# Decoder trunk on one core: where the first layer's mixer issues its modulation steps

## The chip, the cores and the metric

One core of one Trainium2 chip. The time is that of one execution in device microseconds (us). TensorE is PE (its weight loads PEld), VectorE DVE, ScalarE ACT, GpSimd POOL, and SP the engine from which nearly all DMA transfers are issued. Every engine, and SP's DMA queue, takes its instructions in the order in which they are written.

## The reference

Two layers on x of 256 tokens x 2048, f32. Per layer, with `mod` a product of a condition vector with a 2048 x 12288 matrix:

```python
mod = silu(c) @ w_ada[l] + b_ada[l]           # 6 x 2048: shift, scale, gate for mixer and FFN
u = x * (1 + sc_m) + sh_m
proj = u @ w_in[l]
y_attn = sliding_window_attention(q, k, v, sinks, cos, sin)   # 16 heads, 4 kv heads, window 128, rotary
y_rwkv = rwkv7_group(proj[..., ATTN_COLS:], ...)              # 16 heads of 64, delta rule with decay
mix = concatenate([y_attn, y_rwkv]) @ w_out[l]
x = layer_norm(alpha * x + gt_m * mix)
u = x * (1 + sc_f) + sh_f
gate, up = split(u @ w_gate_up[l])
x = layer_norm(alpha * x + gt_f * ((silu(gate) * up) @ w_down[l]))
```

## The kernel before

**Streams.** Every weight is read once, in slabs of 128 rows x 1024 (or 512) columns. A slab is loaded into `raw` (L372), ACT casts its rounded part `hi` (L380), DVE takes the remainder `lo` (L381), and PE multiplies in three products (L402, L403, L405 into `acc`, or L414 to L416 with the operands turned). PE's order is: projection `w_in`, `w_out`, `w_gate_up`, `w_down`, then the second layer.

**Modulation steps.** The matrix `w_ada` (2 x 2048 x 12288) isn't multiplied on PE, except for a small first part. It is worked off in 20 units of 1024 columns, each of 16 steps and three empty turns. A step is one load of 128 x 1024 f32 (512 KB) into `ast`, which has two buffers (L253), and one DVE instruction that multiplies by a scalar per partition and adds to `aacc` (L257, the first of a unit L255). After the 16 steps and two empty turns the unit is summed over partitions: eight PE transposes (L277), eight ACT instructions that add up rows (L281), one DVE instruction (L284) that writes `mods`; gates are written out too (L289). The units are in a fixed order over both layers, and what is not taken in one place is taken in the next.

Steps are drawn from this list in three ways: `pump()` at each weight slab, at `AP[l]` (mixer), `AO[l]` (output projection) and `AF_[l]` (FFN) steps a slab; `adv(n)` at given places, n at a time: `AR` for each of the four chunks of a recurrence, `AA` for each of the 12 operations of attention; and `need()`, which draws what is still wanted before its use.

**The mixer's order.** It is written out in `ORDER`, one string a layer. The RWKV heads are in four groups (0 to 3): D decays, R projection, A preparation (L627 to L720: `ssb` L644, `rs` L647, `rb` L654, `aa` L681, `am` L684, `ax` L692, `at` L699, `kb` L710), I inverse (L723 to L757), C recurrence (L760 to L830), E close. The inverse goes through DRAM: `am` is written to `nscr`, read as `nb` (L727), inverted in 16 x 16 blocks on POOL (L733, L735), written to `tinv` (L738), read as `tm` (L741), then refined in two levels, each of `ytr` (DVE, L745), a product (PE, L749), `yx`, and a product (PE, L756). Q is the projection of q, k, v, X a swap of buffers; a, b and c are attention's rotate, weigh and gather for each kv head (`qk` L888, `ra` L894, `rb` L895, `qr`; scores, softmax `pr` L932; sums into `yl` L460); w and z give the finished columns to `w_out`. For the first layer:

```python
"D0 R0 A0 D1 I0 R1 C0 E0 Q1 A1 I1 D2 R2 A2 Q0 D3 C1 R3 E1 I2 A3 X Q2 a0 a1 b0 C2 a2 b1 c0 E2 a3 c1 I3 b2 b3 c2 c3 w0 C3 w1 w2 E3 z0 z1 z2 z3 w3"
```

The program is then put through a list scheduler that gives each engine its final order by its own estimate of times; so an edit in one place can turn the order of instructions far from it. In the first layer the recurrences 0 and 1 lie beside weight slabs of the projection; 2 and 3 and attention lie mostly behind the last of these slabs.

Of the kernel before, what the change touches and what calls it, by code (L numbers as in the profile page):

```python
# [45 lines left out]
LAG = 2  # L46
WB = (4, 3, 2)
RED = 1
AR = (3, 7)
AA = (1, 45)  # L50
AP = (0.65, 0.3)
AO = (1.1, 2.9)
AF_ = (0.75, 0.55)
# [14 lines left out]
def hybrid_trunk_kernel(  # L68
# [21 lines left out]
    def bank(name="mb", tag="mb"):  # L90

        if tag == "cb":
            return ps.tile([P, 512], F32, tag="cb", name=name)
        t = f"m{turn[0]}"
        turn[0] ^= turn[1]
        return ps.tile([P, 512], F32, tag=t, name=name, bufs=1)
# [241 lines left out]
    def adv(n):  # L338
        for _ in range(n):
            next(ada_rest, None)  # L340
# [149 lines left out]
    def mixer(l, us, mixp, feeds):  # L490
# [71 lines left out]
        def have_y(kts):  # L562
            for k in kts:
                if ys[k] is None:
                    yf = pool_of("ysc").tile([P, T], F32, tag="ysc", name="yf", bufs=1)
                    dma(yf, yd[l, k])
                    ys[k] = split_y(yf)
# [192 lines left out]
        def recur(g, st):  # L760
# [43 lines left out]
            sb = [None, None]  # L804
            H2 = [slice(64 * h, 64 * h + 64) for h in range(2)]
            for cc in range(NCH):
                adv(AR[l])
                o = cc * P
                if cc > 0:
                    for i in I2:  # L810
                        PE.matmul(ob[BH[i], o:o + P], lhsT=st[i]["rh"][:, cc - 1, :], rhs=sb[i], start=True, stop=False)
                for h in range(2):
                    for i in I2:
                        PE.matmul(ob[BH[i], o + h * CH:o + (h + 1) * CH], lhsT=st[i]["am"][h][:, cc, CH:],
                                  rhs=st[i]["uv"][:, cc, H2[h]], start=(cc == 0), stop=(cc == 0 or h == 1))
                if cc == NCH - 1:
                    break
                db = bank("db", "cb")
                for i in I2:
                    for h in range(2):  # L820
                        PE.matmul(db[H2[h], i * CH:(i + 1) * CH], lhsT=st[i]["bkt"][:, cc, H2[h]], rhs=st[i]["uv"][:, cc, H2[h]],
                                  start=True, stop=(cc == 0))
                    if cc > 0:
                        for h in range(2):
                            PE.matmul(db[H2[h], i * CH:(i + 1) * CH], lhsT=st[i]["mt"][:, cc - 1, H2[h]], rhs=sb[i][:, H2[h]],
                                      start=False, stop=True)
                sn = states[turn_s[0]]
                turn_s[0] ^= 1
                for h in range(2):
                    S.copy(sn[H2[h], :, H2[h]], db[H2[h], 0:2 * CH].rearrange("p (i s) -> p i s", i=2))  # L830
                sb = [sn[:, i, :] for i in I2]
# [183 lines left out]
        for op in ORDER[l].split():  # L1015
# [3 lines left out]
            if op[0] == "D":  # L1019
                st[n] = decays(n)  # L1020
            elif op[0] == "R":
                bks[n] = project(n)
            elif op[0] == "A":
                nscr[n] = prepare(n, st[n], bks[n])
            elif op[0] == "I":
                invert(n, st[n], nscr[n])
            elif op[0] == "C":
                recur(n, st[n])
            elif op[0] == "E":
                close(n, st[n])  # L1030
            elif op[0] == "Q":
                project_qkv((AW, 0, 512)[n])
            elif op[0] == "X":
                if not COEX[l]:
                    pa_cm.__exit__(None, None, None)
                    pt_cm, pt = open_pt()
            elif op[0] == "a":
                rotate(n)
            elif op[0] == "b":
                weigh(n)  # L1040
            elif op[0] == "c":
                gather(n)
            elif op[0] == "w":
                add_attention([2 * n, 2 * n + 1], op == ORDER[l].split()[-1])
            elif op[0] == "z":
                add_heads(n, op == ORDER[l].split()[-1])
            if op[0] in "abc":
                adv(AA[l])
        have_y(range(KT))
# [302 lines left out]
```

## Time and profile before

| | |
|---|---|
| three runs | 2692.5, 2694.9, 2695.86 us; median 2694.9 |
| profiled execution | 2694.28 us, of which the span 2692.6 |
| mean granted TensorE clock | 0.965 |
| busy share PE, DVE, ACT, POOL | 93%, 68%, 44%, 5% |
| share of the 16 DMA engines' time taken by SP's transfers (q1) | 71.6% |
| first layer's attention, first `ra` to last `yl` | 448.8 to 537.5 us |
| second layer's | 1772.1 to 1844.9 us |

A busy time is the sum over an engine's instructions. Matmuls overlap in the profile, so their ends are modelled. A bracket behind an instruction gives the idle time of its engine just before it, and what ended it; `x2` joins two alike. A link of the chain is the instruction, transfer or wait that the next one needed last.

### The profile page before, as it was taken

The numbers are of one execution on the slowest core, as the hardware profiler recorded it, in microseconds if no ns is written. First come the engines' busy times: TensorE is split into PE (matmuls) and PEld (weight loads), VectorE is DVE, ScalarE is ACT, GpSimd is POOL, SyncE is SP. The second block draws the span as 40 slices with busy tenths as digits, with TensorE's granted clock in tenths as the row PEclk, the third lists the DMA queues.
The fourth block names the chain that finished last, engine by engine and source line by source line (L and its number), as shares of the span: only waits on it lengthen the run. The fifth ranks groups of instructions, "written<-read, shape, count | busy, mean of one in ns | idle before, by whom it ended". The sixth has DMA issues, their size and how long they took to land.

```text
span 2692.6 us, 41752 instructions
## 1 busy us (share of the span) xinstructions
PE 2501.1 (93%) x15325; PEld 2093.1 (78%) x15325; DVE 1841.0 (68%) x2469; ACT 1188.3 (44%) x2029; POOL 135.0 (5%) x355
## 2 busy tenths in 40 slices
PE   3788998788999999999999999979899999999997
PEld 2687886567888888888889877867688888888887
DVE  6866767979877777777788677555764545545456
ACT  2364452435444444444445544534444444344442
POOL 1002112000000000000000022110000000000000
PEclk9789998899999999999999999989999999999999
DMA  9968668688998888889878586424756656666654
GB/s 315 381 188 253 198 191 238 180 317 296 353 330 309 297 303 312 293 295 308 308 263 304 174 259 188 117 72 144 253 172 188 190 186 196 195 189 189 193 188 149
DMA packets 351999, 637.49 MB, mean 237 GB/s; under 512 B 75894, under 2 KB 142898, under 8 KB 350258
## 3 DMA queue, kind: packets, MB, share of 16 engines
q1 hardware_dynamic: 351794, 634.82, 71.6%
q8 instruction: 120, 1.97, 0.3%
q14 instruction: 85, 0.70, 0.1%
HBM read 622.08 MB, written 12.62 MB: 236 GB/s over the span
## 4 chain that ended last, share of the span: by engine, by line
PE 68%; DMA 8%; DVE 6%; ACT 2%; issue 1%; POOL 1%; SPq 0%; DVEq 0%; POOLq 0%; ACTq 0%
PE acc L403 19%; PE acc L402 19%; PE acc L405 19%; DMA ast<-in_w_ada_dram 3%; DVE aacc L257 2%; PE acc L414 2%; PE acc L415 2%; PE acc L416 2%; DVE lo L381 1%; DMA raw<-in_w_gate_up_dram 1%; PE mb L1225 1%; DMA raw<-in_w_out_dram 1%; DMA yf<-yd 1%; PE mb L277 1%; ACT pr L947 0%
## 5 line engine op out<-in xcount | busy, mean ns | idle before, releaser
L380 ACT CAST hi<-raw 128x1024 fp32r<-128x1024 f32 (+2 forms) x728 | 758.5, 1044 | 1110.8 <-PE acc L405 833.1
L381 DVE TENSOR_TENSOR lo<-raw,hi 128x1024 fp32r<-128x1024 f32 (+2 forms) x728 | 880.2, 1212 | 519.8 <-PE acc L403 347.1
L403 PE MATMUL acc<-lo,u 128*128 128x512 f32 x1568 | 513.4, 395 | 11.9 <-DVE lo L381 11.8
L405 PE MATMUL acc<-hi,u 128*128 128x512 f32 x1568 | 505.8, 391 | 0.0
L257 DVE SCALAR_TENSOR_TENSOR aacc<-ast,cond,aacc 128x1024 f32<-128x1024 f32 x300 | 384.1, 1280 | 127.8 <-DMA ast<-in_w_ada_dram 126.6
L402 PE MATMUL acc<-hi,u 128*128 128x512 f32 x1568 | 457.2, 393 | 0.9 <-ACT u L360 0.5
L403 PEld LDWEIGHTS acc<-lo,u 128*128 128x128 f32 x1568 | 293.8, 189 | 76.4 <-DVE lo L381 16.2
L402 PEld LDWEIGHTS acc<-hi,u 128*128 128x128 f32 x1568 | 294.9, 188 | 63.4 <-ACT sg L1218 0.9
L405 PEld LDWEIGHTS acc<-hi,u 128*128 128x128 f32 x1568 | 295.2, 188 | 61.8 <-issue 0.5
L403 PE MATMUL acc<-lo,ht 128*128 128x512 f32 (+1 forms) x720 | 243.6, 377 | 3.0 <-DVE lo L381 2.9
L405 PE MATMUL acc<-hi,ht 128*128 128x512 f32 (+1 forms) x720 | 242.2, 375 | 0.0
L414 PE MATMUL acc<-u,hi 128*128 128x256 f32 x720 | 206.1, 293 | 14.0 <-ACT hi L380 14.0
L402 PE MATMUL acc<-hi,ht 128*128 128x512 f32 (+1 forms) x720 | 217.0, 376 | 0.0
L415 PE MATMUL acc<-u,hi 128*128 128x256 f32 x720 | 204.5, 291 | 0.0
L416 PE MATMUL acc<-u,lo 128*128 128x256 f32 x720 | 193.1, 294 | 7.1 <-DVE lo L381 7.1
L403 PEld LDWEIGHTS acc<-lo,ht 128*128 128x128 f32 x720 | 135.0, 188 | 29.3 <-DVE lo L381 5.6
L414 PEld LDWEIGHTS acc<-u,hi 128*128 128x128 f32 x720 | 141.9, 197 | 19.3 <-ACT hi L380 14.9
L405 PEld LDWEIGHTS acc<-hi,ht 128*128 128x128 f32 x720 | 135.6, 188 | 24.2
L402 PEld LDWEIGHTS acc<-hi,ht 128*128 128x128 f32 x720 | 134.8, 188 | 24.4
L415 PEld LDWEIGHTS acc<-u,hi 128*128 128x128 f32 x720 | 141.7, 197 | 2.6 <-issue 1.6
L416 PEld LDWEIGHTS acc<-u,lo 128*128 128x128 f32 x720 | 133.8, 197 | 11.6 <-DVE lo L381 9.0
L1067 POOL TENSOR_TENSOR brs<-brs,mhalf 128x1 f32<-128x1 f32 x8 | 7.6, 955 | 1698.7 <-DVE brs L1066 772.1
(349 smaller groups left out, 2901.1 us busy)
## 6 DMA issues: line engine op xcount, KB each, us to landing
ast<-in_w_ada_dram SPq DMA_DIRECT2D x368, 512.0 KB
raw<-in_w_gate_up_dram SPq DMA_DIRECT2D x704, 256.0 KB
raw<-in_w_down_dram SPq DMA_DIRECT2D x176, 512.0 KB
raw<-in_w_in_dram SPq DMA_DIRECT2D x82, 512.0 KB
raw<-in_w_out_dram SPq DMA_DIRECT2D x64, 512.0 KB
raw<-in_w_in_dram SPq DMA_DIRECT2D x120, 256.0 KB
ast<-in_w_ada_dram SPq DMA_DIRECT2D x32, 256.0 KB
lnw<-in_ln_w_dram SPq DMA_DIRECT2D x4, 1024.0 KB
```

The source lines that it names most:

```text
L257: ins = V.scalar_tensor_tensor(acc, t, cond[:, j:j + 1], acc, ALU.mult, ALU.add)
L277: PE.transpose(b[:, i * P:(i + 1) * P], blocks[q + i], ident)
L380: S.copy(h, fl)
L381: ins = V.tensor_tensor(r, fl, h.bitcast(F32), ALU.subtract)
L402: PE.matmul(bt, lhsT=xh, rhs=hi[:, c0:c0 + w], start=st, stop=False)
L403: PE.matmul(bt, lhsT=xh, rhs=lo[:, c0:c0 + w], start=False, stop=False)
L405: PE.matmul(banks[t][q][:, 0:w], lhsT=xl, rhs=hi[:, c0:c0 + w], start=False, stop=sp_)
L414: PE.matmul(bt, lhsT=hi[:, c0:c0 + w], rhs=xh, start=st and opens, stop=False)
L415: PE.matmul(bt, lhsT=hi[:, c0:c0 + w], rhs=xl, start=False, stop=False)
L416: PE.matmul(bt, lhsT=lo[:, c0:c0 + w], rhs=xh, start=False, stop=sp_ and closes)
L1067: G.tensor_tensor(rs[:, 0:1], rs[:, 0:1], mhalf[:, 0:1], ALU.pow)
L1225: PE.transpose(b[:, i * T + t * P:i * T + (t + 1) * P], hh[t][:, (2 * k2 + i) * P:(2 * k2 + i + 1) * P], ident)
```

## The change

In the first layer, each chunk of recurrences 0 and 1 draws six steps in place of three, and each chunk of recurrences 2 and 3 none. Attention's operations draw none in place of one. In the second layer nothing of this changes: seven for each chunk, 45 for each attention operation (by then the list is empty).

```diff
-AR = (3, 7)
-AA = (1, 45)
+AR = ((6, 6, 0, 0), (7, 7, 7, 7))
+AA = (0, 45)
...
             for cc in range(NCH):
-                adv(AR[l])
+                adv(AR[l][g])
```

So these places of the first layer draw 12 + 12 + 12 + 12 and 12 steps before, 24 + 24 + 0 + 0 and 0 after: 48 for 60. The list counts empty turns too. By the program's order, the counts of DVE steps (320 in all) ahead of some places are, before and after: `uv` (L780) of the recurrences 0 to 3 23, 32, 48, 68 and 23, 43, 64, 69, first `ra` 50 and 66, end of attention 79 and 69, first norm 98 and 89, and in the second layer `uv` of recurrence 0 311 and 297. Of PE's rows, 378 matmuls stand between the last one of the second layer's projection and the first of its `w_out` before, 540 after. On DVE in the second layer, group 1's `rs` stood 25 rows ahead of recurrence 0's `uv` (L780), and now stands 28 rows behind it.

SP, first layer, at the start of attention: `nb`, `tinv` and `tm` are group 3's inverse, `qk` and `vt` the rotation's operands, `qkv` the projection's result. Before:

```order
L727 DMA nb<-nscr 64x16x16
L253 DMA ast<-in_w_ada_dram 128x1024 x2
L888 DMA qk<-qkv 128x2x256
L889 DMA qk<-qkv 128x2x64
L876 DMA qkv<-stg 128x512
L890 DMA vt<-qkv 128x2x64 x2
L253 DMA ast<-in_w_ada_dram 128x1024
L890 DMA vt<-qkv 128x2x64
L253 DMA ast<-in_w_ada_dram 128x1024
```

and, five rows further on, after another `qk`, `L738 DMA tinv_154<-ttl 64x8x16 x2`. After:

```order
L253 DMA ast<-in_w_ada_dram 128x1024
L727 DMA nb<-nscr 64x16x16 x2
L253 DMA ast<-in_w_ada_dram 128x1024 x2
L738 DMA tinv_154<-ttl 64x8x16 x2
L741 DMA tm<-tinv_154 64x8x64 x2
L888 DMA qk<-qkv 128x2x256
L889 DMA qk<-qkv 128x2x64
L876 DMA qkv<-stg 128x512
L890 DMA vt<-qkv 128x2x64 x2
```

The inverse's way through `tinv` and `tm` moved ahead of the rotation's first load.

DVE at the same place: the rows at the second rotation before, where group 3's first `ytr` stands (the first rotation's `ra` is ten rows above):

```order
L894 TENSOR_TENSOR ra<-qk,cosk 128x640
L895 TENSOR_TENSOR rb<-qk,sink__147 128x640
L898 TENSOR_TENSOR qr<-ra,rb 128x5x32
L899 TENSOR_TENSOR qr<-ra,rb 128x5x32
L898 TENSOR_TENSOR qr<-ra,rb 128x5x32
L899 TENSOR_TENSOR qr<-ra,rb 128x5x32
L257 SCALAR_TENSOR_TENSOR aacc<-ast,cond,aacc 128x1024
L854 TENSOR_TENSOR sq<-os__4848,vr 128x512
L257 SCALAR_TENSOR_TENSOR aacc<-ast,cond,aacc 128x1024
L745 STREAM_TRANSPOSE ytr<-tm 128x512
```

and the rows at the first rotation after:

```order
L798 TENSOR_TENSOR mt<-mr,mt 128x256
L800 TENSOR_TENSOR rh<-mr,ar 128x192
L720 TENSOR_TENSOR bv<-bnb,vx 128x256
L745 STREAM_TRANSPOSE ytr<-tm 128x512
L255 TENSOR_SCALAR aacc<-ast,cond 128x1024
L257 SCALAR_TENSOR_TENSOR aacc<-ast,cond,aacc 128x1024
L894 TENSOR_TENSOR ra<-qk,cosk 128x640
L895 TENSOR_TENSOR rb<-qk,sink__147 128x640
```

`ytr` moved from behind the second rotation to ahead of the first.

PE, second layer, at the end of the projection (L402, L403, L405 with `u` are its matmuls; L769 to L825 are a recurrence). Before, its last rows, and what follows:

```order
L402 MATMUL acc<-hi,u 128x512
L403 MATMUL acc<-lo,u 128x512
L405 MATMUL acc<-hi,u 128x512
L718 MATMUL bnb<-xr,bones 128x256
L769 MATMUL ta<-atl,tm 64x64 x7
L775 MATMUL tk<-uv,tm 64x64 x16
L784 MATMUL mr<-bkt,ah 128x128 x2
L791 MATMUL mr<-am,ah 64x64 x6
```

After, the last `L405 MATMUL acc<-hi,u 128x512` is followed by the rest of recurrence 1 and some sums, 19 rows, and then:

```order
L845 MATMUL gb<-gda,g2a 128x256
L846 MATMUL gb<-gdb,g2b 128x256
L277 MATMUL mb<-ident,aacc 128x128 x4
L644 MATMUL ssb<-bones,kkn 64x2 x8
L289 MATMUL mb<-ident,mods_136 8x128
L654 MATMUL rb<-ident,rs 64x64 x16
L858 MATMUL oc<-ident,sq 128x128 x4
L681 MATMUL aa<-ar,bkc 128x128 x8
L749 MATMUL m_16800<-ytr,am 64x64 x10
L681 MATMUL aa<-ar,bkc 128x128 x4
```

Group 3's preparation (L644, L654, L681) and the inverse of group 2 (L749) moved from among the projection's matmuls to behind the last of them.

## The prediction

> **What bounds the kernel now.** I read the page's totals first, then the chain that ended last, then the windows around the two places where the edit changes how many steps run, and there the chain and the timelines of single engines.
>
> ```profile
> span 2692.6 us, 41752 instructions
> PE 2501.1 (93%) x15325; PEld 2093.1 (78%) x15325; DVE 1841.0 (68%) x2469; ACT 1188.3 (44%) x2029; POOL 135.0 (5%) x355
> PE 68%; DMA 8%; DVE 6%; ACT 2%; issue 1%; POOL 1%; SPq 0%; DVEq 0%; POOLq 0%; ACTq 0%
> L257 DVE SCALAR_TENSOR_TENSOR aacc<-ast,cond,aacc 128x1024 f32<-128x1024 f32 x300 | 384.1, 1280 | 127.8 <-DMA ast<-in_w_ada_dram 126.6
> ```
>
> PE is busy for 93% and carries 68% of the chain, so where weight slabs stream, a step (one load of `ast`, one DVE instruction of 1.28 us) hides behind matmuls. DMA and DVE carry 14% of the chain; those are the stretches without a stream. The windows (columns: length, then PE, PEld, DVE, ACT and POOL busy, the granted clock, DMA share, GB/s) show which:
>
> ```profile
> 447.00:540.00 93.00, 68.82 (x668) 52.30 (x666) 82.37 (x210) 40.69 (x146) 10.32 (x11) 0.82 0.66 191
> 1772.00:1843.00 71.00, 58.82 (x574) 44.48 (x574) 44.78 (x170) 30.07 (x107) 2.79 (x5) 0.79 0.08 22
> 1730.00:1763.00 33.00, 33.00 (x359) 26.95 (x357) 18.72 (x29) 11.37 (x15) 9.06 (x30) 1.00 0.43 117
> 1763.00:1772.00 9.00, 3.72 (x73) 3.03 (x72) 2.94 (x7) 1.52 (x5) 0.00 (x0) 0.97 0.81 236
> 1600.00:1660.00 60.00, 53.92 (x578) 44.85 (x577) 46.42 (x72) 26.43 (x56) 17.77 (x34) 0.94 0.71 213
> ```
>
> The first two rows are the same stage, attention beside the last recurrences, in the first and the second layer. The first layer's has steps in it: DVE is busy 82.37 of 93 us and PE only 68.82. The second layer's has none: PE is busy 58.82 of 71. Row three is the end of the second layer's projection, where PE has no gap; row four is the wait behind it, PE 3.72 of 9. Row five lies around the second layer's first recurrence.
>
> **The change, part by part.** *First layer, last two groups and attention.* Here 12+12 steps of recurrences 2 and 3 and 12 of attention go, and 24 are added to recurrences 0 and 1, so that 12 fewer run in this layer's mixer, and the program order leaves 3 steps between the first rotation and attention's end. Cost of the 29 steps in the window, from the groups of its lines, and three of the chain's links there (start, length, link):
>
> ```profile
> L257 DVE SCALAR_TENSOR_TENSOR aacc<-ast,cond,aacc 128x1024 f32<-128x1024 f32 x29 | 37.1, 1281 | 10.2 <-DMA ast<-in_w_ada_dram 10.1
> 419.76 5.15 DMA ast<-in_w_ada_dram
> 448.93 5.83 DMA ast<-in_w_ada_dram
> 538.62 1.28 DVE aacc L257
> ```
>
> The steps take 37.1 us of DVE and 10.2 of waits, and their loads are links of the chain. How much of that is on the path is told by the stage's length with and without steps, from the first `ra` (rotation) to the last `yl` of attention, in the DVE timeline (start, length):
>
> ```profile
> 448.82 0.83 DVE L894 TENSOR_TENSOR ra<-qk,cosk 128x640 f32<-128x640 f32 x1
> 537.08 0.41 DVE L460 TENSOR_TENSOR yl<-acc,yl 128x256 fp32r<-128x256 f32 x1
> 1772.07 0.82 DVE L894 TENSOR_TENSOR ra<-qk,cosk 128x640 f32<-128x640 f32 x1 [0.49 <-DMA qk<-qkv]
> 1844.46 0.42 DVE L460 TENSOR_TENSOR yl<-acc,yl 128x256 fp32r<-128x256 f32 x1 [0.44 <-ACT yl L459]
> ```
>
> First layer 537.49 − 448.82 = 88.7 us; second layer 1844.88 − 1772.07 = 72.8. So the most that the removed steps can give is 88.7 − 72.8 = 15.9 us. I don't count on it, since with the steps gone the order turns at the stage's head. Before, SP issues the rotation's `qk` ahead of the last group's `tinv` and `tm` (the inverse, through DRAM), and DVE does `ra` ahead of `ytr`; now `tinv` and `tm` come ahead of `qk`, and `ytr`, which waits for `tm`, ahead of every `ra` (SP's rows in the section on the change). So attention starts when that inverse has come back from DRAM:
>
> ```profile
> 439.55 0.42 SPq L888 DMA_DIRECT2D qk<-qkv  x1
> 451.48 1.72 SPq L738 DMA_DIRECT2D tinv<-ttl  x2
> 427.34 1.28 DVE L684 TENSOR_TENSOR am<-aa,amask 128x512 f32<-128x512 f32 x2
> 464.27 0.71 DVE L745 STREAM_TRANSPOSE ytr<-tm 128x512 f32<-128x512 f32 x1
> 1741.34 1.29 DVE L684 TENSOR_TENSOR am<-aa,amask 128x512 f32<-128x512 f32 x2 [2.32 <-PE aa L681]
> 1770.87 0.71 DVE L745 STREAM_TRANSPOSE ytr<-tm 128x512 f32<-128x512 f32 x1 [4.94 <-DMA tm<-tinv]
> ```
>
> From `am`'s end to `ytr`'s start this group takes 464.27 − 428.62 = 35.7 us; the second layer's takes 1770.87 − 1742.63 = 28.2. By the first, `ytr` ends at 464.98, by the second at 457.5. I take 463, nearer to the group's own row. Then 72.8 us of attention, and the three steps that remain, 3 × 1.28 = 3.8 (estimates): 539.6 against 537.5, **+2**. Ends: 457.5 + 72.8 = 530.3 (−7), and 464.98 + 76.6 + 5.83 for one step's load in the path = 547.4 (+10). Queued behind the waiting `ytr` are all of the rotation, and behind that PE's scores.
>
> *First layer, recurrences 0 and 1.* Each issues 12 steps more, while a stream runs. SP has room there, and PE has a gap from a late `lo`:
>
> ```profile
> 356.90 1.12 SPq L372 DMA_DIRECT2D raw<-in_w_in_dram  x2
> 370.89 1.28 SPq L738 DMA_DIRECT2D tinv<-ttl  x2
> 379.72 0.38 PE L416 MATMUL acc<-u,lo 128*128 128x256 f32 x1 [2.55 <-DVE lo L381]
> ```
>
> The 12.9 us between the first two are free for loads. The new order has `lo` ahead of `ytr`, so that gap can go (−2.5); recurrence 0 stands some 1 us longer with 12 × 1.28 = 15.4 us more on DVE in front of its chain's end. Sum **−1.5**, ends −2.5 and +5 (four steps uncovered, 4 × 1.28).
>
> *First layer's FFN.* With 10 steps less behind it, the modulation unit for the second half of the FFN's input is summed inside the FFN's first stream, not ahead of the norm. ACT's part (same window, groups of lines):
>
> ```profile
> L281 ACT ACTIVATE mb<-mb 128x128 f32<-128x128 f32 x12 | 3.2, 263 | 4.9 <-PE mb L277 4.8
> L281 ACT ACTIVATION_READ_ACCUMULATOR mb<-mb 128x1 f32 x12 | 2.3, 190 | 0.0
> ```
>
> 8 × (263 + 190) ns = 3.6 us of ACT, while PE has the first half's matmuls: **+2**, ends 0 and +5 (3.6 and one more step's 1.28).
>
> *Second layer.* Ten of the twelve steps come back here, and by the order 23 instead of 9 lie beside its first recurrence, while the stream runs. In the fifth window DVE has 46.42 us busy of 60; 14 × 1.28 = 17.9 more make 64.3, 4.3 too many. Nor does DMA hide them: 60 us × 213 GB/s plus 14 × 0.524 MB is 20.1 MB, 335 GB/s, which is above what this window in another stream reached:
>
> ```profile
> 640.00:700.00 60.00, 55.32 (x246) 44.03 (x247) 53.70 (x72) 38.55 (x69) 1.30 (x2) 0.93 0.86 296
> ```
>
> At 296 GB/s it is 67.9, +7.9. I take **+5** for the stream, ends 0 and +12.9 (17.9 with 5 covered).
>
> The greater part is order. Before, group 1's preparation (DVE `rs`) stood ahead of recurrence 0; now it stands behind it with steps between, ten weight slabs later, and all behind it follows: group 3's preparation and two levels of group 2's inverse stood among the projection's matmuls, and now stand behind the last of them (PE's rows in the section on the change). 378 matmuls stood between the projection's last one and the first of w_out; now 540. The chain before, at the place where they hid (x counts loads and matmuls), and from DVE's timeline the start of the preparation and the end of a rotation:
>
> ```profile
> 1727.62 1.02 PE ssb L644 x16
> 1736.48 1.42 PE aa L681 x16
> 1728.65 1.08 PE m L749 x32
> 1728.69 0.17 DVE L647 TENSOR_SCALAR rs<-ssb 64x16 f32<-64x16 f32 x1 [0.52 <-PE ssb L644]
> 1774.38 0.32 DVE L899 TENSOR_TENSOR qr<-ra,rb 128x160 f32<-128x160 f32 x1
> ```
>
> The stream loses 162 small matmuls; at 58.82 us / 574 = 0.102 us each (the window of 1772) that is 16.6 us, and its end moves from 1763 to 1763 − 16.6 + 5 = 1751.4. From group 3's `rs` to `ytr` it was 1770.87 − 1728.69 = 42.2 us, beside a PE without a gap; now that chain begins where the stream ends: 1793.6. Two of the four rotations now come ahead of `ytr`; one took 1774.70 − 1772.07 = 2.6 us, so the stage gets −5.3: its start is at 1788.3 as against 1772.07, **+16.2** with the stream's +5 in it. Ends: with this stream gone the chain could go as fast as 42.2 − 16.6 = 25.6, which gives 0; with the tail of recurrence 1 and of group 2's inverse, some ten links of 1.08, in front of it, and the stream's upper end 7.9 more, 16.2 + 10.8 + 7.9 = +35. I take the middle, since the chain's own links are DVE, DMA and PE in turn, and only PE's lose their company.
>
> *Sum:* −1.5 + 2 + 2 + 16.2 = +18.7 on the profiled execution's 2694.28 us (span 2692.6), which is 0.6 under the median 2694.9: **2713 us**.
>
> [...] The windows give the clock as 0.79 where PE was busy 58.82 of 71 us and 1.00 where it had no gap. [...]
>
> GpSimd's part of the last group's inverse, in its timeline:
>
> ```profile
> 446.59 0.22 POOL L733 TENSOR_TENSOR tmp<-nb,ttl 128x21 f32<-128x21 f32 x1
> 447.75 1.22 POOL L733 TENSOR_TENSOR tmp<-nb,ttl 128x14 f32<-128x14 f32 x1
> 447.62 1.28 DVE L257 SCALAR_TENSOR_TENSOR aacc<-ast,cond,aacc 128x1024 f32<-128x1024 f32 x1
> ```
>
> The second took 1.22 us for fewer elements, and ended only when the step beside it did. [...]
>
> **The rivals.** *Faster: the first layer's tail is freed.* If `ytr` is not what attention waits for (the point: `ytr` ending by 449), the stage takes 72.8 us from 448.82 and ends at 521.6, −15.9; with no loss in the second layer, its tail's shorter chain making up for the moved work, and +2 at the FFN: 2680. For it: DVE's 82.37 of 93 us and the links of `ast`. Against: the orders on SP and DVE, and that the inverse took 28 us even without steps. *Same:* the second layer gives 0, its lower end, and the first −1.5 + 2 + 2: 2697. *Slower still:* the 14 steps of the second layer's stream are not covered at all, 17.9 instead of 5: 2726; for it, the `ast` waits that total 126.6 us on the page; against, that these lie mostly where PE runs on. That the edit does nothing is excluded: the rows moved on every engine.
>
> **How the numbers follow.** About 0.2% (5.4 us) is what a measurement of this kernel can tell from no change. Forecast (2703 to 2724) 0.58; slower still 0.12; same 0.12; faster 0.18. So slower 0.70. The range leaves out the faster case and reaches from 2686 (the first layer's lower end −7 with the second at 0) to 2730 (slower still and some more at the FFN).
>
> **What would show it.** After: first `ra` of the first layer at about 463 behind `ytr`, attention's end at 535 to 547; PE with one wait or several of 15 to 25 us in sum behind the second layer's last projection matmul, then attention of about 73 us. Wrong it would be if `ra` starts before 452, if attention ends before 528, or if the time from the first layer's end to the second layer's first w_out slab does not grow.

## The result, and the profile after

The changed kernel takes 2741.2 us (median of four runs, 2737.1 to 2749.4) against 2693.7: ratio 1.0178, interval 1.0163 to 1.0194. It is slower, as forecast, but by 47 us where 19 were forecast, and outside the range (2686 to 2730). The profiled execution took 2737.09 us, 42.8 more than the one before; all stages below are read from these two executions.

The page's totals:

```profile
span 2735.4 us, 41759 instructions
PE 2524.9 (92%) x15325; PEld 2109.7 (77%) x15325; DVE 1842.2 (67%) x2469; ACT 1188.1 (43%) x2029; POOL 134.3 (5%) x355
```

The same work is done: DVE is busy for the same time, and PE's busy time is 23.8 us more for the same 15325 matmuls. The rest is waiting and order. How late the changed kernel is at some places (start of an instruction in the timeline, after less before):

| place | before, us | late by |
|---|---|---|
| 51st `lo` of all (first layer, before recurrence 0) | 257.3 | −3.2 |
| 81st `lo` (first layer's projection, near its end) | 413.0 | +14.5 |
| end of attention (last `yl` from `acc`) | 537.5 | +4.5 |
| first residual of `w_out`, L1144 | 588.5 | +8.1 |
| second norm, third L1067 | 1400.4 | +12.3 |
| second layer, first `ra` | 1772.1 | +38.9 |
| its first residual, L1144 | 1889.7 | +44.8 |
| end of span | 2692.6 | +42.8 |

So the first layer loses 12.3 us (14.5 and more in its projection, of which attention gives back 10), and the second 30.5.

*The first layer's projection.* DVE's groups for the stretch from recurrence 0 to just behind the 81st `lo`, in the kernel before and in the changed one (busy time, mean ns, idle before and what ended it); the stretch is 275 to 420 us before, 275 to 435 after:

```profile
L381 DVE TENSOR_TENSOR lo<-raw,hi 128x1024 fp32r<-128x1024 f32 x30 | 36.3, 1214 | 11.1 <-PE acc L416 10.7 <-issue 0.4
L257 DVE SCALAR_TENSOR_TENSOR aacc<-ast,cond,aacc 128x1024 f32<-128x1024 f32 x21 | 26.7, 1270 | 2.5 <-DMA ast<-in_w_ada_dram 2.4
```

```profile
L257 DVE SCALAR_TENSOR_TENSOR aacc<-ast,cond,aacc 128x1024 f32<-128x1024 f32 x36 | 46.0, 1276 | 19.2 <-DMA ast<-in_w_ada_dram 18.9
L381 DVE TENSOR_TENSOR lo<-raw,hi 128x1024 fp32r<-128x1024 f32 x29 | 35.2, 1216 | 6.0 <-ACT hi L380 3.4 <-PE acc L416 2.6
```

Fifteen steps more are 19.3 us more of DVE and 16.5 us more of waits for their loads. Before, DVE waited 10.7 us for PE to free the next `lo`, that is PE was the bound; after, 2.6. SP's queue over 275 to 435, first before, then after (total wait, times, longest; for the kernel before this reaches 15 us past its stretch, and up to 420 its two rows are 44.1 and 8.8):

```profile
SPq L372 <- DVE lo L381: 45.6, 22, 6.8
SPq L253 <- DVE aacc L257: 11.1, 12, 1.7
```

```profile
SPq L253 <- DVE aacc L257: 26.4, 23, 2.8
SPq L372 <- DVE lo L381: 24.0, 17, 3.6
```

The weight loads (L372) used to wait 45.6 us in all for a free buffer; by so much they were ahead of DVE, which is called their lead here. Now the step's load (L253) waits 26.4 us for one of its two buffers, and the weights queue behind it; their lead is 24.0.

*The first layer's attention*, the windows and DVE's rows of its start:

```profile
435.00:470.00 35.00, 20.66 (x286) 17.03 (x284) 16.73 (x23) 9.13 (x30) 7.04 (x30) 0.82 0.59 173
470.00:542.00 72.00, 61.46 (x568) 46.10 (x570) 49.81 (x177) 31.07 (x112) 3.75 (x5) 0.78 0.20 61
```

```profile
467.66 0.71 DVE L745 STREAM_TRANSPOSE ytr<-tm 128x512 f32<-128x512 f32 x1 [12.69 <-DMA tm<-tinv]
470.24 0.82 DVE L894 TENSOR_TENSOR ra<-qk,cosk 128x640 f32<-128x640 f32 x1
541.55 0.42 DVE L460 TENSOR_TENSOR yl<-acc,yl 128x256 fp32r<-128x256 f32 x1 [0.44 <-ACT yl L459]
```

DVE waits 12.69 us at `ytr`, with the rotation behind it, and attention then takes 541.97 − 470.24 = 71.7 us, nearly the 72.8 of a stage without steps.

*The second layer.* The windows of the stream from the 440th `lo` on, and of the stretch behind it up to `ra`, before and after:

```profile
1572.00:1760.00 188.00, 178.56 (x1864) 150.43 (x1864) 124.39 (x198) 87.97 (x188) 45.49 (x112) 0.96 0.60 175
1760.00:1772.00 12.00, 6.72 (x127) 5.42 (x125) 5.03 (x9) 3.43 (x8) 0.00 (x0) 0.98 0.71 195
```

```profile
1594.00:1763.00 169.00, 158.69 (x1446) 133.67 (x1446) 118.17 (x162) 73.00 (x147) 26.88 (x67) 0.96 0.70 218
1763.00:1811.00 48.00, 34.52 (x421) 28.07 (x419) 16.00 (x35) 16.36 (x46) 8.70 (x31) 0.77 0.25 63
```

The stream became shorter, with 418 matmuls fewer in it, and the stretch behind it holds 294 more and grew from 12 to 48 us, in which DVE is busy a third. In PE's and then DVE's timeline of the changed kernel:

```profile
1763.02 0.39 PE L405 MATMUL acc<-hi,u 128*128 128x512 f32 x1
1767.65 0.44 PE L811 MATMUL ob<-state,rh 128*64 128x128 f32 x4 [1.54 <-ACT state L830]
1773.06 0.66 PE L277 MATMUL mb<-ident,aacc 128*128 128x128 f32 x4
1775.38 1.87 PE L644 MATMUL ssb<-bones,kkn 128*64 128x2 f32 x16 [1.66 <-ACT mb L281]
```

```profile
1777.28 0.17 DVE L647 TENSOR_SCALAR rs<-ssb 64x16 f32<-64x16 f32 x1 [1.76 <-PE ssb L644]
1811.00 0.82 DVE L894 TENSOR_TENSOR ra<-qk,cosk 128x640 f32<-128x640 f32 x1 [7.30 <-DMA qk<-qkv]
1819.66 0.70 DVE L745 STREAM_TRANSPOSE ytr<-tm 128x512 f32<-128x512 f32 x1
1883.56 0.42 DVE L460 TENSOR_TENSOR yl<-acc,yl 128x256 fp32r<-128x256 f32 x1 [0.44 <-ACT yl L459]
```

After the last projection matmul (1763.41) come 13.9 us of recurrence 1's chunks and a step unit's sum, then group 3's chain from `rs` to `ytr`, 42.4 us, with `ra` 8.7 us ahead of its end; then attention, 73.0 us.

### The profile page after: what moved, and what is told of

It reads as the page before. It is cut to its first block, busy times and chain, and to the rows that moved or that the text cites. A ratio compares the mean times of both kernels' runs of the same rounds, so it can differ in the third digit from the quotient of the medians.

```text
span 2735.4 us, 41759 instructions
## 1 busy us (share of the span) xinstructions
PE 2524.9 (92%) x15325; PEld 2109.7 (77%) x15325; DVE 1842.2 (67%) x2469; ACT 1188.1 (43%) x2029; POOL 134.3 (5%) x355
## 5 line engine op out<-in xcount | busy, mean ns | idle before, releaser
L403 PE MATMUL acc<-lo,u 128*128 128x512 f32 x1568 | 514.6, 395 | 11.3 <-DVE lo L381 11.2
L405 PE MATMUL acc<-hi,u 128*128 128x512 f32 x1568 | 507.3, 392 | 0.0
L402 PE MATMUL acc<-hi,u 128*128 128x512 f32 x1568 | 458.6, 394 | 0.5 <-ACT u L360 0.5
L403 PEld LDWEIGHTS acc<-lo,u 128*128 128x128 f32 x1568 | 294.9, 189 | 79.0 <-DVE lo L381 18.0
L405 PEld LDWEIGHTS acc<-hi,u 128*128 128x128 f32 x1568 | 296.1, 189 | 62.0 <-issue 0.5
L402 PEld LDWEIGHTS acc<-hi,u 128*128 128x128 f32 x1568 | 295.3, 189 | 62.1 <-issue 1.0
L403 PE MATMUL acc<-lo,ht 128*128 128x512 f32 (+1 forms) x720 | 243.8, 377 | 3.3 <-DVE lo L381 3.1
L405 PE MATMUL acc<-hi,ht 128*128 128x512 f32 (+1 forms) x720 | 242.2, 375 | 0.0
L414 PE MATMUL acc<-u,hi 128*128 128x256 f32 x720 | 206.7, 294 | 17.9 <-ACT hi L380 16.5
L402 PE MATMUL acc<-hi,ht 128*128 128x512 f32 (+1 forms) x720 | 217.2, 376 | 0.0
L414 PEld LDWEIGHTS acc<-u,hi 128*128 128x128 f32 x720 | 142.8, 199 | 23.7 <-ACT hi L380 17.8
L403 PEld LDWEIGHTS acc<-lo,ht 128*128 128x128 f32 x720 | 135.0, 188 | 30.6 <-DVE lo L381 7.3
L405 PEld LDWEIGHTS acc<-hi,ht 128*128 128x128 f32 x720 | 135.6, 188 | 24.4
L402 PEld LDWEIGHTS acc<-hi,ht 128*128 128x128 f32 x720 | 134.7, 188 | 24.2
L1067 POOL TENSOR_TENSOR brs<-brs,mhalf 128x1 f32<-128x1 f32 x8 | 7.6, 956 | 1689.3 <-DVE brs L1066 777.0
```

The lines of the kernel that those rows point to most:

```text
L402: PE.matmul(bt, lhsT=xh, rhs=hi[:, c0:c0 + w], start=st, stop=False)
L403: PE.matmul(bt, lhsT=xh, rhs=lo[:, c0:c0 + w], start=False, stop=False)
L405: PE.matmul(banks[t][q][:, 0:w], lhsT=xl, rhs=hi[:, c0:c0 + w], start=False, stop=sp_)
L414: PE.matmul(bt, lhsT=hi[:, c0:c0 + w], rhs=xh, start=st and opens, stop=False)
L1067: G.tensor_tensor(rs[:, 0:1], rs[:, 0:1], mhalf[:, 0:1], ALU.pow)
```

## Experiments

"Theory 1" to "3" in the expectations: 1, the second layer's loss comes of the turned order; its rival, of the 14 steps more beside recurrence 0; 3, dense steps in recurrences 0 and 1 cost 18 us. The table gives each run's median, the ratio to the kernel before on the same chip with its interval, and from the profiles how late the second norm is (first layer) and what is added from there to the end of the span (second layer). "Left" is the number of steps not yet done at the second layer's recurrence 0 (9 before), and "tail" the matmuls between the projection's last one and the FFN's first there, in rows of the program (909 before; where an expectation speaks of `w_out`'s stream with such a number, this count is meant).

| run | us | ratio (interval) | first layer | second layer | left | tail |
|---|---|---|---|---|---|---|
| changed | 2741.2 | 1.0178 (1.0163 to 1.0194) | +12.3 | +30.5 | 23 | 1102 |
| e_back80 | 2709.5 | 1.0046 (1.0032 to 1.0060) | +19.4 | −1.5 | 9 | 915 |
| e_less70 | 2720.6 | 1.0088 (1.0065 to 1.0112) | −0.8 | +29.4 | 22 | 1094 |
| e_ar_only | 2714.6 | 1.0073 (1.0051 to 1.0095) | +25.3 | +0.4 | 9 | 909 |
| e_aa_only | 2730.5 | 1.0124 (1.0103 to 1.0145) | +5.0 | +32.1 | 23 | 1102 |
| e_tail_free | 2759.4 | 1.0235 (1.0213 to 1.0258) | +42.8 | +24.5 | 23 | 915 |
| e_front_only | 2727.3 | 1.0124 (1.0110 to 1.0138) | +38.3 | −5.4 | 0 | 915 |
| e_a1_first | 2729.0 | 1.0122 (1.0104 to 1.0140) | +17.2 | +20.6 | 32 | 1007 |
| e_tf88 | 2736.4 | 1.0157 (1.0139 to 1.0176) | +57.6 | −10.1 | 0 | 915 |
| h_a | 2709.2 | 1.0041 (1.0026 to 1.0057) | +13.8 | +2.6 | few in the mixer | 926 |
| h_b | 2700.1 | 1.0019 (1.0011 to 1.0028) | −2.6 | +6.9 | few | 926 |
| h_c | 2693.4 | 0.9997 (0.9985 to 1.0008) | −6.6 | +5.1 | few | 928 |
| h_d | 2692.3 | 0.9983 (0.9974 to 0.9992) | −3.5 | +6.7 | few | 925 |
| i_a | 2683.4 | 0.9958 (0.9945 to 0.9971) | −4.2 | −2.7 | few | 919 |

**The two layers apart.** e_back80 gives the 12 steps back in the first layer's FFN (changed kernel, one number):

```diff
-AF_ = (0.75, 0.55)
+AF_ = (0.80, 0.55)
```

> The changed kernel with the FFN of the first layer drawing 0.80 instead of 0.75 steps a slab, so that the 12 steps saved in its mixer are issued there and the second layer's mixer has its old order (group 1's preparation ahead of recurrence 0, 9 steps left). Theory 1 (two separate losses: about 14 us in the first layer, about 29 in the second, the second from the turned order or the steps there): +10 to +18 us against before, the second layer's time from its first recurrence to its end as before within 3 us. Rival (the second layer loses because the first one hands over late or otherwise): +38 to +48 as in the changed kernel.

e_less70 takes the kernel before and leaves 12 steps over for the second layer:

```diff
-AF_ = (0.75, 0.55)
+AF_ = (0.70, 0.55)
```

> The kernel before with the first layer's FFN drawing 0.70 instead of 0.75 steps a slab: the first layer's mixer is untouched, about 12 steps more are left for the second layer's mixer, whose order turns as in the changed kernel. Theory 1: +22 to +32 us, all of it in the second layer's mixer. Rival (the loss is made in the first layer and carried on): -3 to +3.

Both as theory 1 had them: +12.4 us by the ratio with the second layer whole, and +23.7 with the first layer untouched. The two losses are separate and about add up: by the ratios to 36 of 48 us, by the profiles (17.9 and 28.6) to 46.5 of 42.8. What the 12 steps do in the second layer doesn't hang on the first layer's mixer.

**The two halves of the edit.** e_ar_only has the new recurrences and the old attention; e_aa_only the reverse:

```diff
-AA = (0, 45)
+AA = (1, 45)
```

> Half of the change: 24, 24, 0, 0 steps in the recurrences, but attention keeps its 12. The second layer's order is as before. Theory 3 (24 steps in each of recurrences 0 and 1 cost 18 us, since SP's queue stands at the two ast buffers in front of the weight slabs): the last lo of the projection's first 80 slabs late by 14 to 20 us, the total +15 to +25. Rival (the steps there are hidden; the loss was made by the turned inverse at the start of attention): up to that point less than 5 us late, the total +5 to +12.

```diff
-AR = ((6, 6, 0, 0), (7, 7, 7, 7))
+AR = ((3, 3, 3, 3), (7, 7, 7, 7))
```

> The other half: recurrences keep 12 steps each, attention draws none. The second layer's order is turned, with the projection's last matmul even farther from w_out's first (1102 matmuls between, 909 before). Theory 1: the first layer's attention ends 3 to 8 us early, the second layer loses 22 to 32; total +15 to +28. Rival (the second layer's loss comes from the first's): -8 to 0.

e_ar_only's 81st `lo` was late by 16.1 us and its total by 19.7: theory 3 holds. e_aa_only lost 33 us, 5 more than the expectation's upper end, and by its profile all but 5 in the second layer. Its first layer's attention ended 3.4 us early, at the low end of the 3 to 8 expected, and at the first residual of `w_out` nothing of that was left (0.5 late).

**Steps taken from the tail, and none added in front.** e_tail_free, and e_tf88 with the FFN's rate raised so that none are left for the second layer:

```diff
-AR = ((6, 6, 0, 0), (7, 7, 7, 7))
+AR = ((3, 3, 0, 0), (7, 7, 7, 7))
```

> Steps 12, 12, 0, 0 in the first layer's recurrences, none in its attention: the tail is as free of steps as in the changed kernel, recurrences 0 and 1 carry no more than before. In the order, ra comes ahead of the last group's ytr again; the second layer has its old order (group 1's preparation ahead of recurrence 0, 915 matmuls behind that stream) but 23 steps beside recurrence 0, as the changed kernel has. Theory 3: the first layer's attention ends 10 to 16 us early. The FFN needs 27 steps more at its start, at most 27 x 1.28 = 35 us of DVE, partly covered: +5 to +20. Theory 1 (the turned order makes the second layer's loss): the second layer loses 0 to 6; total -10 to +10. Rival (the 14 steps beside recurrence 0 make it): the second layer loses 20 to 30, total +15 to +35.

```diff
-AR = ((6, 6, 0, 0), (7, 7, 7, 7))
-AF_ = (0.75, 0.55)
+AR = ((3, 3, 0, 0), (7, 7, 7, 7))
+AF_ = (0.88, 0.55)
```

> As the run with 12, 12, 0, 0 and none in attention, and the first layer's FFN draws 0.88 steps a slab, so that the second layer's order and its steps are those of before. Theories 1 and 3: attention of the first layer 10 to 16 us early, the FFN's start 5 to 20 late, the FFN 0 to +5, second layer 0; total -10 to +10. If the total is below -5, it beats both kernels.

The tail itself does give what the prediction's faster rival said: the first residual comes 17.5 us early (21.3 in e_tf88). But the modulation for the FFN's input is then late, and PE stands still for it. e_tail_free's PE timeline:

```profile
662.02 1.94 PE L277 MATMUL mb<-ident,aacc 128*128 128x128 f32 x8 [9.08 <-DVE aacc L257]
705.47 1.94 PE L277 MATMUL mb<-ident,aacc 128*128 128x128 f32 x8 [41.51 <-DVE aacc L257]
```

This was sized at +5 to +20; it cost 57 (−16.2 us at the first norm, +41.2 at the 131st `lo`, in the FFN's first stream). So the totals, +63 and +42, missed every expectation. And theory 1 failed: with the old order but 23 steps, the second layer lost 24.5 us, as the rival had it.

**Only added in front:**

```diff
-AR = ((6, 6, 0, 0), (7, 7, 7, 7))
-AA = (0, 45)
+AR = ((6, 6, 3, 3), (7, 7, 7, 7))
+AA = (1, 45)
```

> Steps 24, 24, 12, 12 and 12 in attention: only the addition, nothing taken away. The second layer's list is empty at its recurrence 0. Theory 3: the stream beside recurrences 0 and 1 late by 14 to 20 us and nothing given back at attention; second layer as before; total +15 to +25. Rival (the steps added there are paid by steps saved later): -3 to +6.

It lost 33 us, more than either had it: +13.2 at the 81st `lo`, then a further 12 in a tail that has steps and the turned `ytr` too.

**The order in the second layer**, with group 1's preparation written ahead of recurrence 0:

```diff
-    "D0 R0 A0 D1 R1 I0 C0 Q2 E0 A1 I1 ...
+    "D0 R0 A0 D1 R1 I0 A1 C0 Q2 E0 I1 ...
```

> The changed kernel with A1 written ahead of C0 in the second layer's order, so that group 1's preparation stands ahead of recurrence 0 although as many steps are left as in the changed kernel. 1007 matmuls between the stream's last and w_out's stream, by the same count 909 before and 1102 as changed. Theory 1: the second layer loses 5 to 15 instead of about 29, total +18 to +30. Rival (steps): total +40 to +48.

The second layer lost 20.6 in place of 30.5, although 32 steps were left at that point: between the two expectations. Order carries a part.

**What a step costs.** In both kernels either DVE's instruction of a step or its load is cut to a sixteenth of its columns; these four kernels leave the modulation incomplete. The load falls from 512 to 32 KB, the DVE instruction only from a mean of 1280 to 281 ns (g_dve_before):

```profile
L257 DVE SCALAR_TENSOR_TENSOR aacc<-ast,cond,aacc 128x64 f32<-128x64 f32 x300 | 84.4, 281 | 133.6 <-DMA ast<-in_w_ada_dram 132.4
```

```diff
-ins = V.scalar_tensor_tensor(acc, t, cond[:, j:j + 1], acc, ALU.mult, ALU.add)
+ins = V.scalar_tensor_tensor(acc[:, 0:64], t[:, 0:64], cond[:, j:j + 1], acc[:, 0:64], ALU.mult, ALU.add)
```

> The kernel before, with the DVE instruction of a step on 64 columns in place of 1024 (its load whole; the modulation is left incomplete). The base for the next run. Some -20 to -90 us against before, since the steps' DVE time is 384 us in all.

> The changed kernel with the same 64 columns. Theory D (a step costs what its DVE instruction takes in DVE's row of work, 1.28 us): against the run before this one the first layer's projection is late by 0 to +4 us at its 80th slab, where the changed kernel had +14.5, and the whole is +15 or less, where it had +43 to +47. Theory Q (a step costs through its 512 KB load and the two buffers in SP's queue, with the weight slabs behind them): +10 to +16 at the 80th slab and +30 to +45 in all.

```diff
-dma(t, src[:, j, n0:n0 + 1024])
+dma(t[:, 0:64], src[:, j, n0:n0 + 64])
...
+# and t[:, 0:64] read 16 times by the DVE instruction
```

> The kernel before, with the load of a step cut to 64 columns (32 KB in place of 512) and DVE's instruction of full width, which reads these 64 columns sixteen times (the modulation is then wrong). The base for the next run; between -5 and -60 us against before.

> The changed kernel with the same small loads. Theory D: against the run before this one +10 to +18 at the 80th slab of the first layer's projection and +30 to +47 in all. Theory Q: 0 to +4 and +15 or less.

Medians 2667.8 and 2680.9 with the small DVE instruction, 2675.1 and 2699.9 with the small load. Changed less before, by the profiles:

| | whole steps | small DVE instruction | small load |
|---|---|---|---|
| 81st `lo` | +14.5 | +4.5 | +7.7 |
| at the second norm | +12.3 | −1.2 | +2.3 |
| second layer | +30.5 | +18.6 | +24.8 |
| median | +47.5 | +13.1 | +24.8 |

Neither theory alone: cutting DVE's time takes away more than cutting the load, though each cut takes a large part. With most of DVE's time gone, 18.6 us stay in the second layer, whose order is turned in that run too (1080 matmuls in the tail).

**Steps out of the second layer's mixer.** Its bursts are set to zero and its output projection draws 0.7 a slab: h_a in the changed kernel; h_b, h_c and h_d in the kernel before, with the first FFN at 0.75, 0.70, 0.65:

```diff
-AR = ((6, 6, 0, 0), (7, 7, 7, 7))
-AA = (0, 45)
-AO = (1.1, 2.9)
+AR = ((6, 6, 0, 0), (0, 0, 0, 0))
+AA = (0, 0)
+AO = (1.1, 0.7)
```

> The changed kernel, and in the second layer no bursts of steps in recurrences and attention; its output projection draws 0.7 in place of 2.9 a slab. Steps are left over for the FFN's stream. Few steps (12) lie in the second layer's whole mixer, and the order there is as before. If the steps that come back make the loss (with the order that they turn): the second layer loses nothing or gains up to 10 us against before, total +0 to +14, what the first layer loses. Rival (what is lost there doesn't hang on the steps): +35 to +48.

> The kernel before, with the second layer's bursts taken out in the same way: first layer and its FFN untouched. 9 to 15 steps move from the second layer's mixer to its output projection and FFN. By a cost of 1 to 2 us a step in the mixer and next to nothing in the FFN's stream: -3 to -12 us. Rival (hidden in the mixer): -2 to +3.

> As the run before this one, with the first layer's FFN at 0.70 steps a slab: 9 steps fewer in it. By the same cost, and 0.4 us for each step less in that FFN: -5 to -15 us. Rival (as the kernel before at 0.70, that lost 26 us): +15 to +26.

> The same with 0.65: 19 steps fewer in the first layer's FFN, and all steps of the second layer's second gate are left for its FFN. -6 to -20 us; rival: the modulation needed ahead of the second layer's FFN comes late and PE waits for its sums, 0 to +20.

In h_a the second layer's loss is gone, and its total is what the first layer loses, +11 us by the ratio. h_b, h_c and h_d were to gain 3 to 20 us; by the ratios h_b lost 5, h_c came out the same and h_d gained 4.6: up to the second layer's first residual they are 8.0, 15.0 and 12.7 us early, and behind the norm 3.6 late, 5.5 and 1.1 early. The gain is lost in the output projection, where steps now lie. i_a takes them out of there as well, on h_c:

```diff
-AO = (1.1, 0.7)
+AO = (1.1, 0.0)
```

> The kernel before with no bursts in the second layer's mixer, 0.70 steps a slab in the first layer's FFN, and none drawn in the second layer's output projection: the last 26 to 30 steps, all of the second layer's last gate, lie in its FFN's stream. If the steps in the output projection gave the gain back: 8 to 18 us faster than before, a version that beats both. Rival (they would cost as much in the FFN's first products): -3 to +3.

2683.4 us against 2694.2, ratio 0.9958: 11 us faster than the kernel before, within the 8 to 18 expected. DVE's group of steps for 1400 to 1900 us, before and in i_a:

```profile
L257 DVE SCALAR_TENSOR_TENSOR aacc<-ast,cond,aacc 128x1024 f32<-128x1024 f32 x44 | 56.3, 1280 | 31.3 <-DMA ast<-in_w_ada_dram 31.1
```

```profile
L257 DVE SCALAR_TENSOR_TENSOR aacc<-ast,cond,aacc 128x1024 f32<-128x1024 f32 x27 | 34.5, 1277 | 3.7 <-DMA ast<-in_w_ada_dram 3.7
```

The last gate's 26 or so steps lie in the second layer's FFN, beside a stream in which the page's slices give DVE 4 to 5 tenths.

## Why the prediction was right or wrong

The direction was right, and the largest place (the second layer) too; the size was not. The sum had +18.7 where the profile gives +42.8. Of the 24.1 us between, 14.3 are the second layer's and 9.8 the first's, which the sum had at +2.5:

- *Recurrences 0 and 1, −1.5 (ends −2.5 and +5): wrong, +14.5 to +18.* The failing step is "SP has room there" with PE's single gap of 2.55 us as the measure. Nor was there room: in those 12.9 us the next row of SP's queue, `tinv`, waited for GpSimd, and the rows behind it with it:

```profile
SPq L738 <- POOL ttl L735: 12.8, 1, 12.8
```

  And room in SP's queue said nothing on DVE, which carries `lo`, the groups' chain and the steps in one row: 15 steps were 19.3 us of it. The small DVE instruction took the delay from 14.5 to 4.5. The step's two buffers in front of the weights have a part too (7.7 with small loads).
- *First layer's tail, +2 (−7 to +10): the mechanism right, the number by luck.* `ytr` ahead of `ra` held the rotation up, attention then took 71.7 us (72.8 forecast), and the end came 4.5 late. But the tail began 14.5 us late and gave back 10. What was mis-sized is the inverse's way: from the end of `am` (443.53) to `ytr` (467.66) it took 24.1 us, where the prediction had 28.2 to 35.7. With GpSimd's last instruction at 450.85 before and 460.99 after (below), SP issued `tm` 7.1 us behind it before and 2.9 after:

```profile
442.85 0.68 DVE L684 TENSOR_TENSOR am<-aa,amask 128x512 f32<-128x512 f32 x1
457.94 1.28 SPq L741 DMA_DIRECT2D tm<-tinv  x2
463.89 1.27 SPq L741 DMA_DIRECT2D tm<-tinv  x2
```

  From the old end of `am`, 428.62, the same 98.4 us would have led to 527 (an estimate), 10 us early and below the stated range; the lateness that the projection handed over covered it. Where `ra` stands first, in e_tail_free and e_tf88, attention ended 21.5 and 24.0 us early, more than the faster rival's 15.9.
- *FFN's start, +2 (0 to +5): right,* +3.6 between the first residual and the 131st `lo`; from 588 to 720 us PE waits 1.2 us for the unit's last step, and 3.1 instead of 1.0 for `lo`. The larger lesson is e_tail_free's 57 us: where the sum was needed before it was done, PE stood still for 9.08 and 41.51 us.
- *Second layer, +16.2 (0 to +35): right in kind, short by 14.3.* Set against the 12.3 with which it begins, its projection ended 9.4 us early (11.6 forecast from 1763; the last matmul before ends at 1760.5), `rs` to `ytr` took 42.4 us (42.2), the rotation came 8.7 ahead (5.3), attention 73.0 (72.8). What failed is "now that chain begins where the stream ends": 13.9 us of recurrence 1 stood between. The text had these links at 10.8 and used them for the upper end alone. Some 4 us more are lost between attention and the end.
- *The stream's end in that term: close by luck.* Two sizes were wrong in opposite directions. The 14 steps more were put at +5; in e_tail_free, with the same 23 steps but the old order, the projection's last matmul comes 21.3 us late against the second norm. (Its last row, and that of the kernel before, with which the 1760.5 is read:)

```profile
1824.21 0.39 PE L405 MATMUL acc<-hi,u 128*128 128x512 f32 x1
1760.07 0.40 PE L405 MATMUL acc<-hi,u 128*128 128x512 f32 x1
```

  And "162 small matmuls" at 0.102 us took rows of the program at the price of the trace's records, where such an f32 product left two (group 3's `ssb` has 8 rows in the order and x16 in the timeline, its `rb` 16 and x32). Between the projection's last matmul and `w_out`'s first, the traces have 676 records before and 987 after. These 311 are 31.9 us at that price, not 16.6, and with them the forecast for the second layer would have been about +1. Changed against e_tail_free, the stream's end is 30.7 us earlier for 299 records; but with the small DVE instruction it is only 9.9 earlier for 313. So how the −9.4 splits between moved work and steps is not shown.
- *The rivals.* "Slower still" had the right mechanism, steps not covered at all, but only for the second layer. Its point against, that the waits for `ast` "lie mostly where PE runs on", was not a reason: PE ran on (busy for 149.61 of 160 us in the first layer's projection), only later. All its 17.9 us would still have fallen short, at 2726.
- *The signs.* Attention's end at 542.0 and the second layer's attention of 73.0 us came as stated. The first `ra` came at 470.2, not 463, and behind the second layer's last projection matmul PE was idle for 13.5 of 48 us, less than the 15 to 25 stated.
- *The order as the cause in the second layer* was put at 11 and the steps at 5. The runs don't split it so. At the old order, 0, 9 and 23 steps left gave −5 and −10, 0 to −1.5, and +24.5; at the turned order 22 and 23 gave 29 to 32; with the small DVE instructions, but whole loads, the turned order gave 18.6. The steps alone cost most of it, and with the turned order it is little more; the order without any cost of the steps was not run. Both begin with the steps: with few of them in the mixer (h_a) the tail is near the old one (926) and the loss is gone.
- *GpSimd and the clock,* for which the sum has no term. GpSimd's part of the last group's inverse, first and last instruction, before and after:

```profile
438.74 0.47 POOL L733 TENSOR_TENSOR tmp<-nb,ttl 128x15 f32<-128x15 f32 x1 [49.82 <-DMA nb<-nscr]
450.56 0.29 POOL L735 TENSOR_TENSOR ttl<-ttl,tmp 128x8 f32<-128x8 f32 x1
```

```profile
451.68 0.21 POOL L733 TENSOR_TENSOR tmp<-nb,ttl 128x15 f32<-128x15 f32 x1 [51.16 <-DMA nb<-nscr]
460.77 0.22 POOL L735 TENSOR_TENSOR ttl<-ttl,tmp 128x8 f32<-128x8 f32 x1
```

12.1 us before, 9.3 after, where DVE stands idle from 454.96 on, beside its last two thirds. The `tmp` of 128x14 that took 1.22 us beside a step (447.75) took 0.21 us after (459.89), with DVE idle. These 2.8 us were not what decided. The new wait in the second layer (1763 to 1811) has a granted clock of 0.77, and over the span the clock fell from 0.965 to 0.958; PE's busy sum is 23.8 us more for the same 15325 matmuls. How much of the time the clock made is not shown by any run here.

Open stays why the stretch from attention's end to the first residual of `w_out` is longer by 3.6 us in the first layer and 5.7 in the second.

## What to carry to other kernels

Background work is priced on each engine that it touches, at the place where it runs: a stream in which PE has no gap may have no room on DVE, and there 15 steps of 1.28 us cost 14.5 to 17.7 us. Put such work by the latest time that it is needed, and look for the stretch with idle DVE and queue, here the second layer's FFN (−0.4%), not for the stretch that looks busiest without it. When a scheduler reorders the program, compare its order far from the edit, and take a new tail's length from the chain's first waiting link, not from the end of the stream ahead of it. Before a count is multiplied by a mean, see that both count the same thing, rows of the program or records of the trace. And a place that comes out at its forecast time has not borne the forecast out until its beginning has been looked at as well.

## What the runs showed of the hardware

Taking 15/16 of the bytes of the steps' loads off gave 17 us in the kernel before and 41 in the changed one; taking 300 of their 384 us of DVE time off gave 25 and 60. So what a resource is worth here hangs on the place where it is used, not on its sum. An engine that reads as busy can still be late, as PE here: busy for 149.61 of 160 us, and 14.5 us late at the 81st `lo`. The windows of the first layer's projection up to the 81st `lo`, before and after:

```profile
275.00:420.00 145.00, 141.14 (x1441) 118.71 (x1439) 104.14 (x162) 70.72 (x140) 24.27 (x68) 1.00 0.67 203
```

```profile
275.00:435.00 160.00, 149.61 (x1436) 125.13 (x1435) 120.69 (x173) 71.14 (x155) 32.38 (x68) 0.96 0.77 234
```

PE does the same 1440 matmuls in 15 us more, and 8.5 of these count as busy.
